# A fourth buffer of split weights, and the tiles that make room for it, in a one-core decoder block

## The chip, the core and the metric

The kernel runs on one core of one Trainium2 chip. The core has a matrix engine (PE; its weight loads are shown apart as PEld), a vector engine (DVE), an activation engine (ACT), a general engine (POOL), and a sync engine whose queue (SP) issues the transfers from memory. Each engine works through its own instructions in the order in which they stand. The metric is the device time of one execution in microseconds (us), the median of several runs. The profiled execution is one more of them, and its trace names start, end and releaser of each instruction.

## The reference: what is computed

One decoder layer over 256 tokens of width 2048, all in float32:

```python
xn = rms_norm(h, norm_mix_g)
proj = xn @ w_in                      # 2048 -> 1024 + 1024 + 3*1024 + 3*2048
u_s5, u_lru, q, k, v, gate_logits = split(proj)
gates = sigmoid(gate_logits + b_gate)
y_s5   = s5_branch(u_s5, ...)         # complex diagonal recurrence, 64 groups x 64 states, GELU, GLU
y_lru  = rglru_branch(u_lru, ...)     # causal conv, two block-diagonal gates, real recurrence
y_attn = stick_breaking_attention(q, k, v)   # 8 heads of 128
merged = g_s5*(y_s5 @ w_br_s5) + g_lru*(y_lru @ w_br_lru) + g_attn*(y_attn @ w_br_attn)
h = h + merged @ w_out
hn = rms_norm(h, norm_mlp_g)
h = h + relu(hn @ w_up)**2 @ w_down   # 2048 -> 8192 -> 2048
return rms_norm(h, final_norm_g)
```

In the S5 branch the state turns by a fixed angle per step, so the kernel needs cosine and sine of (frequency x step) for 256 steps of each state.

## The kernel before, in words

**Units.** All large weights are read once, as a stream of 520 units. A unit is 256 rows by 512 columns of one weight matrix, 512 KB, held in a tile of 128 partitions by 1024 elements. `stream` lists them in the order of their use: first `w_in` for the LRU and S5 inputs, then gates and branch products, attention inputs, the S5 tail with `w_glu`, `w_out`, and last `w_up` and `w_down`.

**Split weights.** To keep float32 accuracy in a faster matmul form, every unit is split in two: ACT casts the raw tile to a rounded `hi` (line 146), DVE subtracts to get `lo` (line 147). Activations are split the same way. A product is then three matmuls: hi by hi, hi by lo, lo by hi. `chunk` (lines 225 to 227) makes the output with channels on the partitions, 24 matmuls of 256 columns per unit; `chunk_tok` (lines 241 to 243) and `pair_tok` (lines 276 to 278) make it with tokens on the partitions, 12 matmuls of 512 columns per unit.

**How far ahead.** `next_unit` is called before the matmuls of unit i. It issues loads up to unit i+3 into one of three `raw` buffers (pool `wraw`), and splits up to unit i+2 into one of three pairs of `hi` and `lo` buffers (pool `whi`). The split of unit i+2 therefore waits until PE has done with unit i-1, whose buffers it takes, and the load of a unit waits until the split of the unit three before it has freed its `raw` buffer. A load waiting in SP's queue holds up everything behind it there.

**Side work.** All else runs between the units. After each unit's matmuls `pump` takes a step of every open side task: the norms, the LRU branch (`lru_half`), the S5 branch (`s5_scan`), attention, the transposes of the feed-forward part. `pump` ties these steps behind the newest split on ACT and DVE and behind the unit's last matmul on PE; within such bounds a scheduler sets each engine's order when the program is built. So the number of splits that stand ahead of a side step on its engine is given by how far ahead the splits are issued.

**The S5 branch.** `s5_params` computes the angles on POOL: a per-state frequency, split in a low part (per step) and a high part (per 16 steps), and from them two tables `flo` and `fhi` of 128 x 32 x 16 each. `s5_scan` goes through 8 blocks of 4 state tiles. For each block it splits the input into `ux`, copies it by 12 small transfers (`s5_stack`, line 627) into `stk`, multiplies (`ps_v`), turns by the tables from `s5_tables` (lines 604 to 611: a DVE sum of `fhi` and `flo`, then ACT and DVE make cosine and sine `tc` and `ts`), scans, turns back, and multiplies again (`ps_y`, line 698). After the eighth block come GELU and the split into `yg_hi` and `yg_lo`, which the `w_glu` chunks read.

**Memory.** Tile pools give out memory. Tiles of one tag share that tag's buffers: a new tile of the tag waits until the old one is released, that is until its last reader is done. `wr` and `wi` (the LRU's block-diagonal gate weights) lie in the LRU's pool, `stk` in the S5 pool, `vt` (attention values) under its own tag, and `x_tok` and `ho` (residual input, output rows) side by side in the feed-forward pool.

Of the kernel before, what the change touches and what calls it, by code (L numbers as in the profile page):

```python
# [9 lines left out]
F32 = mybir.dt.float32  # L10
F32R = mybir.dt.float32r
AF = mybir.ActivationFunctionType
ALU = mybir.AluOpType
# [33 lines left out]
def hybrid_block(ctx: ExitStack, tc: tile.TileContext, io, out):  # L47
# [2 lines left out]

    const = ctx.enter_context(tc.tile_pool(name="const", bufs=1))
    wraw = ctx.enter_context(tc.tile_pool(name="wraw", bufs=3))
    whi = ctx.enter_context(tc.tile_pool(name="whi", bufs=3))
    act = ctx.enter_context(tc.tile_pool(name="act", bufs=1))
    ypool = ctx.enter_context(tc.tile_pool(name="ypool", bufs=2))
    tmp = ctx.enter_context(tc.tile_pool(name="tmp", bufs=2))
# [94 lines left out]
    def next_unit():  # L151
        i = st["use"]
        st["use"] += 1
        while st["load"] <= min(i + 3, len(stream) - 1):
            load_next()
            load_x(st["load"])
        while st["split"] <= min(i + 2, len(stream) - 1):
            before_split(st["split"])
            split_next()
        return (stream[i], *hi.pop(i))  # L160
# [147 lines left out]
    bco = sp.tile([P, WT, 2, 64], F32, name="bco")  # L308
    ce = sp.tile([P, 2, 32, 2, 16], F32, name="ce")
    ux = sp.tile([P, 4, L], F32R, name="ux")  # L310
    stk = sp.tile([96, NT, 2, L], F32R, name="stk")
    rad = sp.tile([P, 32], F32, name="rad")
    fhi = sp.tile([P, 32, 16], F32, name="fhi")
    flo = sp.tile([P, 32, 16], F32, name="flo")
    pp = s5.enter_context(tc.tile_pool(name="s5w", bufs=1))


# [94 lines left out]
    def s5_params():  # L412
        lr, li, dt, a, b, n, w, den, sh, ch, ea, em, xr, xi, cr, ci = (prm[:, k, :] for k in range(16))
        g = nc.gpsimd
        g.memset(ce, 0.0)
        for _ in range(9):
            yield
        nc.scalar.activation(dt, dt, AF.Exp)
        yield
        g.tensor_tensor(b, li, dt, ALU.mult)  # L420
        g.tensor_tensor(a, lr, dt, ALU.mult)
        g.tensor_scalar(n, b, 1.0 / TWO_PI, MAGIC, ALU.mult, ALU.add)
        g.tensor_scalar(n, n, -MAGIC, None, ALU.add)
        for cst in (PI_A, PI_B, PI_C):
            g.tensor_scalar(w, n, cst, None, ALU.mult)
            g.tensor_tensor(b, b, w, ALU.subtract)
        g.tensor_scalar(b, b, math.pi, -math.pi, ALU.min, ALU.max)
        yield
        g.tensor_scalar(w, b, 1.0 / TWO_PI, None, ALU.mult)
        g.tensor_scalar(n, w, 16.0, MAGIC, ALU.mult, ALU.add)  # L430
        g.tensor_scalar(n, n, -MAGIC, None, ALU.add)
        g.tensor_scalar(cr, w, 16.0, None, ALU.mult)
        g.tensor_tensor(n, cr, n, ALU.subtract)
        sb = steps.unsqueeze(1).broadcast_to([P, 32, 16])
        g.tensor_tensor(flo, w.unsqueeze(2).broadcast_to([P, 32, 16]), sb, ALU.mult)
        g.tensor_tensor(fhi, n.unsqueeze(2).broadcast_to([P, 32, 16]), sb, ALU.mult)
        yield
        nc.scalar.activation(ch, b, AF.Abs)
        nc.scalar.activation(sh, b, AF.Sin, scale=0.5)
        nc.scalar.activation(ch, ch, AF.Sin, scale=-0.5, bias=half_pi)  # L440
        nc.scalar.activation(ea, a, AF.Exp)
        nc.scalar.activation(em, a, AF.Tanh, scale=0.5)
        g.tensor_tensor(den, lr, lr, ALU.mult)
        g.tensor_tensor(w, li, li, ALU.mult)
        g.tensor_tensor(den, den, w, ALU.add)
        yield
        nc.vector.reciprocal(den, den)
        g.tensor_scalar(n, sh, 2.0, None, ALU.mult)
        g.tensor_tensor(xi, n, ch, ALU.mult)
        g.tensor_tensor(w, ea, em, ALU.mult)  # L450
        g.tensor_tensor(em, em, w, ALU.add)
        g.tensor_scalar(rad, em, 1.0, None, ALU.add)
        g.tensor_tensor(n, n, sh, ALU.mult)
        g.tensor_tensor(n, n, ea, ALU.mult)
        g.tensor_tensor(xr, em, n, ALU.subtract)
        g.tensor_tensor(xi, xi, ea, ALU.mult)
        yield
        g.tensor_tensor(cr, xr, lr, ALU.mult)
        g.tensor_tensor(w, xi, li, ALU.mult)
        g.tensor_tensor(cr, cr, w, ALU.add)  # L460
        g.tensor_tensor(cr, cr, den, ALU.mult)
        g.tensor_tensor(ci, xr, li, ALU.mult)
        g.tensor_tensor(w, xi, lr, ALU.mult)
        g.tensor_tensor(ci, ci, w, ALU.subtract)
        g.tensor_tensor(ci, ci, den, ALU.mult)
        yield
        cb_, ib_ = (x.unsqueeze(2).broadcast_to([P, 32, 16]) for x in (cr, ci))
        for k, (p, q, op) in enumerate(((cb_, ib_, ALU.add), (ib_, cb_, ALU.subtract))):
            u = pp.tile([P, 2, 32, 16], F32, tag="ts", name=f"cq{k}", bufs=2)
            nc.vector.tensor_tensor(u[:, 0], cco[:, 0], p, ALU.mult)  # L470
            yield
            nc.vector.tensor_tensor(u[:, 1], cco[:, 1], q, ALU.mult)
            yield
            for h in range(2):
                r_ = slice(64 * h, 64 * h + 64)
                nc.vector.tensor_tensor(ce[r_, k, :, h, :], u[r_, 0], u[r_, 1], op)
                yield
# [14 lines left out]
    nsp8 = const.tile([P, WT], F32, name="nsp8")  # L492
    tiny = const.tile([P, 1], F32, name="tiny")
    nc.gpsimd.memset(tiny, 2.0 ** -115)
    wr = lp.tile([P, WT, P], F32, name="wr")
    wi = lp.tile([P, WT, P], F32, name="wi")
    for t, src in ((wr, "lru_w_r"), (wi, "lru_w_i")):
        nc.gpsimd.memset(t, 0.0)

# [95 lines left out]
    def s5_tables(b):  # L595
        c = pp.tile([P, NT, 16, 16], F32, tag="tc", name=f"tc{b}", bufs=2)
        s = pp.tile([P, NT, 16, 16], F32, tag="ts", name=f"ts{b}", bufs=2)
        q = slice(b * NT, (b + 1) * NT)
        sh = [P, NT, 16, 16]
        f = "p n a b -> p (n a b)"  # L600
        cf, sf = c.rearrange(f), s.rearrange(f)

        def gen():
            nc.vector.tensor_tensor(c, fhi[:, q, :].unsqueeze(3).broadcast_to(sh), flo[:, q, :].unsqueeze(2).broadcast_to(sh), ALU.add)
            yield
            nc.scalar.activation(sf, cf, AF.Identity, bias=magic)
            nc.vector.scalar_tensor_tensor(sf, sf, -MAGIC, cf, ALU.add, ALU.subtract)
            yield
            nc.scalar.activation(cf, sf, AF.Abs)
            nc.scalar.activation(sf, sf, AF.Sin, scale=-TURN)  # L610
            nc.scalar.activation(cf, cf, AF.Sin, scale=-TURN, bias=half_pi)
            yield
        f = "p n a b -> p n (a b)"
        return (c.rearrange(f), s.rearrange(f)), gen()

    def s5_split(ct):
        bx = [ux[:, 2 + i, :].rearrange("p (r g s) -> p r g s", r=2, g=2) for i in range(2)]
        nc.scalar.copy(ux[:, 0, :], us5[:, ct, :])
        nc.vector.tensor_tensor(ux[:, 1, :], us5[:, ct, :], ux[:, 0, :].bitcast(F32), ALU.subtract)
        for g in range(2):  # L620
            m = mask[:, g:g + 1]
            nc.scalar.activation(bx[0][:, :, g, :], bco[:, ct], AF.Copy, scale=m)
            nc.vector.scalar_tensor_tensor(bx[1][:, :, g, :], bco[:, ct], m, bx[0][:, :, g, :].bitcast(F32), ALU.mult, ALU.subtract)

    def s5_stack(t):
        for i, w_ in enumerate((ux[:, 0:4:2, :], ux[:, 1:3, :], ux[:, 0:4:3, :])):
# [4 lines left out]
    def s5_scan():  # L631
# [12 lines left out]
        for b in range(WT):  # L644
# [11 lines left out]
            if b + 1 < WT:  # L656
                s5_split(b + 1)
                tabs, more = s5_tables(b + 1)
                yield
            tt(t1, vr, c, ALU.mult)  # L660
            yield
            tt(t2, vi, s, ALU.mult)
# [172 lines left out]
    for c in range(2):  # L835
        kT = ap_.tile([P, 4, L], F32, tag="k", name=f"kT{c}")
        banks = chunk("w_in", 6 + c, D, xs)
        for j in range(2):
            scaled(kT[:, 2 * j:2 * j + 2, :], banks[j])
        qT = ap_.tile([P, 4, L], F32, tag="q", name=f"qT{c}")  # L840
        banks = chunk("w_in", 4 + c, D, xs)
        for j in range(2):
            nc.vector.scalar_tensor_tensor(qT[:, 2 * j:2 * j + 2, :], v2(banks[j]), P ** -0.5, rstd2, ALU.mult, ALU.mult)
        vbox = [None]
        tasks.append(later([attention(range(4 * c, 4 * c + 4), kT, qT, vbox)], 1.0))
        banks = chunk_tok("w_in", 8 + c, D, xs)
        vt = ap_.tile([P, 2, CH], F32, tag="v", name=f"vt{c}")
        for t in range(2):
            nc.scalar.activation(vt[:, t, :], banks[t], AF.Copy, scale=rstd_tok[:, t:t + 1])
        vbox[0] = vt  # L850
        if c == 0:
            finish(tasks[0])
# [67 lines left out]

    mlp = ctx.enter_context(tc.tile_pool(name="mlp", bufs=1))
    gp = small("norm_mlp_g")
    x_tok = mlp.tile([P, 2, D], F32, name="xres")

    def x_load():
        for c in range(4):
# [71 lines left out]


    gfb = mlp.tile([P, D], F32, name="gfb")  # L1000
    ho = mlp.tile([P, 2, D], F32, name="ho")
    ssq = mlp.tile([P, 2, 6], F32, name="ssq")
    rf = mlp.tile([P, 2], F32, name="rf")

# [166 lines left out]
```

## Time and profile before

| what | value |
|---|---|
| median of 3 runs | 1511.09 us (1510.91 to 1512.21) |
| the profiled execution: time, and span of its trace | 1512.1 us, 1510.3 us |
| mean granted PE clock over the span | 0.995 |
| PE busy | 1488.4 us, 99% |
| DVE busy | 1175.2 us, 78% |
| ACT busy | 782.3 us, 52% |
| POOL busy | 35.3 us, 2% |
| bytes moved, mean rate | 292.41 MB, 194 GB/s |

Busy PE means that a matmul is on its way, from its start to its modelled end; matmuls overlap, so the mean duration of one (389 ns for 512 columns) is longer than the distance from one to the next. A stall shows as idle time of PE and of PEld with its releaser, and as a gap between starts. The granted clock is a share of full speed: a stretch at 0.86 ran its matmuls as if 14% of it were lost.

### The profile page before, as it was taken

Reading aid. Unit: us, or ns where it says so; the run is one execution under the profiler, and the core shown is the slowest. Engines: PE = TensorE matmul, PEld = TensorE weight load, DVE = VectorE, ACT = ScalarE, POOL = GpSimd, SP = SyncE. Lnnn points to the kernel's source line nnn. Section 1 sums busy time; section 2 is a strip of 40 time slices with the busy share of each in tenths; the row PEclk is TensorE's granted clock in tenths of the full one; section 3 lists DMA queues with packets and bytes.
Section 4 is the critical chain, followed back from the end, with each engine's and each line's share of the span. In section 5 each row is a group of like instructions: output and inputs, shape, how many; then the busy total and the mean of one; then the engine's idle time right before and its main releaser. Section 6 shows DMA issues by size and latency. Waiting matters only on the chain.

```text
span 1510.3 us, 19900 instructions
## 1 busy us (share of the span) xinstructions
PE 1488.4 (99%) x7518; PEld 1260.5 (83%) x7518; DVE 1175.2 (78%) x1468; ACT 782.3 (52%) x920; POOL 35.3 (2%) x60
## 2 busy tenths in 40 slices
PE   9999999999999999999999999999999999999997
PEld 9997788989887878988887888888888888888886
DVE  6767998897988989689799796568854787558965
ACT  6767556565765564544455544344433444344443
POOL 1400000000000000000000000000000000000011
PEclk9999999999999999999999999999999999999999
DMA  9546766665555666666855666666666666666664
GB/s 287 157 153 176 228 205 201 187 182 168 175 172 183 208 182 210 189 202 190 276 182 188 197 184 205 194 185 196 198 194 193 193 195 195 195 191 191 192 197 152
DMA packets 89858, 292.41 MB, mean 194 GB/s; under 512 B 12834, under 2 KB 17058, under 8 KB 89634
## 3 DMA queue, kind: packets, MB, share of 16 engines
q1 hardware_dynamic: 89618, 291.07, 62.6%
q8 instruction: 59, 0.97, 0.3%
q14 instruction: 37, 0.30, 0.1%
q10 hardware_dynamic: 144, 0.07, 0.0%
HBM read 282.71 MB, written 2.10 MB: 189 GB/s over the span
## 4 chain that ended last, share of the span: by engine, by line
PE 83%; DVE 9%; issue 3%; ACT 2%; DMA 2%; SPq 0%; DVEq 0%; ACTq 0%
PE mt_w_up L242 6%; PE mt_w_up L241 6%; PE mt_w_up L243 6%; PE mt_w_in L242 5%; PE mt_w_in L243 5%; PE mt_w_in L241 5%; PE mt_w_down L242 4%; PE mt_w_down L241 4%; PE mt_w_down L243 4%; PE mp_w_down L277 4%; PE mp_w_down L278 4%; PE mp_w_down L276 4%; PE mm_w_in L227 4%; PE mm_w_in L225 4%; PE mm_w_in L226 4%; DVE lo L147 3%
## 5 line engine op out<-in xcount | busy, mean ns | idle before, releaser
L146 ACT CAST hi<-raw 128x1024 fp32r<-128x1024 f32 (+1 forms) x521 | 545.2, 1049 | 625.9 <-PE mt_w_up L243 131.4
L147 DVE TENSOR_TENSOR lo<-raw,hi 128x1024 fp32r<-128x1024 f32 (+1 forms) x521 | 637.9, 1225 | 287.7 <-ACT hi L146 284.1
L242 PE MATMUL mt_w_in<-lo,xhi 128*128 128x512 f32 x448 | 176.1, 393 | 3.9 <-DVE lo L147 3.7
L241 PE MATMUL mt_w_in<-hi,xhi 128*128 128x512 f32 x448 | 175.2, 396 | 0.2 <-ACT hi L146 0.2
L243 PE MATMUL mt_w_in<-hi,xlo 128*128 128x512 f32 x448 | 175.2, 391 | 0.0
L241 PE MATMUL mt_w_up<-hi,hhi 128*128 128x512 f32 x448 | 174.3, 389 | 0.0
L242 PE MATMUL mt_w_up<-lo,hhi 128*128 128x512 f32 x448 | 174.3, 389 | 0.0
L243 PE MATMUL mt_w_up<-hi,hlo 128*128 128x512 f32 x448 | 174.3, 389 | 0.0
L227 PE MATMUL mm_w_in<-xhi,lo 128*128 128x256 f32 x512 | 145.4, 286 | 4.5 <-DVE lo L147 4.5
L225 PE MATMUL mm_w_in<-xhi,hi 128*128 128x256 f32 x512 | 146.5, 286 | 0.5 <-ACT hi L146 0.4
L226 PE MATMUL mm_w_in<-xlo,hi 128*128 128x256 f32 x512 | 145.7, 285 | 0.0
L728 DVE STREAM_TRANSPOSE reluT<-relu 32x256 f32<-32x256 f32 x256 | 111.5, 436 | 4.2
L242 PEld LDWEIGHTS mt_w_in<-lo,xhi 128*128 128x128 f32 x448 | 84.6, 189 | 24.0 <-DVE lo L147 7.6
L227 PEld LDWEIGHTS mm_w_in<-xhi,lo 128*128 128x128 f32 x512 | 98.7, 194 | 5.5 <-DVE lo L147 5.5
L242 PE MATMUL mt_w_down<-lo,hd_hi 128*128 128x512 f32 (+1 forms) x272 | 102.5, 377 | 0.0
L241 PE MATMUL mt_w_down<-hi,hd_hi 128*128 128x512 f32 (+1 forms) x272 | 102.4, 377 | 0.0
L243 PE MATMUL mt_w_down<-hi,hd_lo 128*128 128x512 f32 (+1 forms) x272 | 102.4, 376 | 0.0
L225 PEld LDWEIGHTS mm_w_in<-xhi,hi 128*128 128x128 f32 x512 | 99.2, 194 | 1.1 <-ACT hi L146 1.0
L277 PE MATMUL mp_w_down<-lo,hd_hi 128*128 128x512 f32 x256 | 99.8, 390 | 0.1
L278 PE MATMUL mp_w_down<-hi,hd_lo 128*128 128x512 f32 x256 | 99.6, 389 | 0.0
L276 PE MATMUL mp_w_down<-hi,hd_hi 128*128 128x512 f32 x256 | 99.6, 389 | 0.0
L241 PEld LDWEIGHTS mt_w_in<-hi,xhi 128*128 128x128 f32 x448 | 84.5, 189 | 17.8 <-ACT hi L146 0.7
(299 smaller groups left out, 2370.2 us busy)
## 6 DMA issues: line engine op xcount, KB each, us to landing
raw<-in_w_in SPq DMA_DIRECT2D x175, 512.0 KB, 4.3
raw<-in_w_up SPq DMA_DIRECT2D x128, 512.0 KB, 4.2
raw<-in_w_down SPq DMA_DIRECT2D x128, 512.0 KB, 4.2
raw<-in_w_out SPq DMA_DIRECT2D x32, 512.0 KB, 4.2
raw<-in_w_br_lru SPq DMA_DIRECT2D x16, 512.0 KB, 4.6
raw<-in_w_br_attn SPq DMA_DIRECT2D x16, 512.0 KB, 4.1
raw<-in_w_br_s SPq DMA_DIRECT2D x16, 512.0 KB, 4.1
stk<-ux SPq DMA_DIRECT2D x96, 64.0 KB, 4.1
```

The costliest lines, as they stand in the source:

```text
L146: anchor["act"] = nc.scalar.copy(h[:, k, :], r[:, k, :]).ins
L147: anchor["dve"] = nc.vector.tensor_tensor(l_[:, k, :], r[:, k, :], h[:, k, :].bitcast(F32), ALU.subtract).ins
L225: nc.tensor.matmul(o, wh[:, kk, s], xh, start=first and ct % 2 == 0, stop=False, skip_group_check=True)
L226: nc.tensor.matmul(o, wh[:, kk, s], xl, start=False, stop=False, skip_group_check=True)
L227: mm = nc.tensor.matmul(o, wl[:, kk, s], xh, start=False, stop=last and ct % 2 == 1, skip_group_check=True)
L241: nc.tensor.matmul(banks[j], xh[:, s], wh[:, a:b], start=kt == 0, stop=False)
L242: nc.tensor.matmul(banks[j], xh[:, s], wl[:, a:b], start=False, stop=False)
L243: return nc.tensor.matmul(banks[j], xl[:, s], wh[:, a:b], start=False, stop=kt == ng * UK - 1)
L276: nc.tensor.matmul(o, xh[:, s], wh[:, kk, :], start=kt == 0, stop=False)
L277: nc.tensor.matmul(o, xh[:, s], wl[:, kk, :], start=False, stop=False)
L278: mm = nc.tensor.matmul(o, xl[:, s], wh[:, kk, :], start=False, stop=kt == ng * UK - 1)
L728: nc.vector.transpose(d_[32 * a:32 * a + 32, :, :, 32 * b:32 * b + 32], s_[32 * b:32 * b + 32, :, :, 32 * a:32 * a + 32])
```

## The change

Six edits.

- The pool `whi` has four pairs of `hi` and `lo` buffers in place of three.
- `next_unit` loads four units ahead in place of three, and splits three ahead in place of two. The pool `wraw` stays at three buffers.
- `wr` and `wi` become halves of one tile `wrwi` in the S5 pool under the tag `stk`, and `stk` is allocated later under the same tag, so it takes this memory once the LRU's last gate matmul has read it.
- `fhi` and `flo` go. Their two frequency columns stay in `fw` (128 x 2 x 32), and for each S5 block POOL multiplies 4 of them by the 16 steps into a tile `ph` (two instructions of 128 x 64 per block), one step of the generator before DVE's sum. So `s5_tables` has one step more.
- `vt` takes the tag of `kT`: it waits for the logits of its four heads, and the next `kT` waits for the products that read `vt`.
- `x_tok` and `ho` share one buffer under the tag `rows`.

```diff
-    whi = ctx.enter_context(tc.tile_pool(name="whi", bufs=3))
+    whi = ctx.enter_context(tc.tile_pool(name="whi", bufs=4))
...
-        while st["load"] <= min(i + 3, len(stream) - 1):
+        while st["load"] <= min(i + 4, len(stream) - 1):
...
-        while st["split"] <= min(i + 2, len(stream) - 1):
+        while st["split"] <= min(i + 3, len(stream) - 1):
...
-    stk = sp.tile([96, NT, 2, L], F32R, name="stk")
-    fhi = sp.tile([P, 32, 16], F32, name="fhi")
-    flo = sp.tile([P, 32, 16], F32, name="flo")
+    fw = sp.tile([P, 2, 32], F32, name="fw")
...
+        w = fw[:, 0, :]
         g.tensor_scalar(w, b, 1.0 / TWO_PI, None, ALU.mult)
...
-        g.tensor_tensor(n, cr, n, ALU.subtract)
-        sb = steps.unsqueeze(1).broadcast_to([P, 32, 16])
-        g.tensor_tensor(flo, w.unsqueeze(2).broadcast_to([P, 32, 16]), sb, ALU.mult)
-        g.tensor_tensor(fhi, n.unsqueeze(2).broadcast_to([P, 32, 16]), sb, ALU.mult)
+        g.tensor_tensor(fw[:, 1, :], cr, n, ALU.subtract)
...
-    wr = lp.tile([P, WT, P], F32, name="wr")
-    wi = lp.tile([P, WT, P], F32, name="wi")
+    wrwi = sp.tile([P, 2, WT, P], F32, tag="stk", name="wrwi")
+    wr, wi = wrwi[:, 0], wrwi[:, 1]
...
-            nc.vector.tensor_tensor(c, fhi[:, q, :].unsqueeze(3).broadcast_to(sh), flo[:, q, :].unsqueeze(2).broadcast_to(sh), ALU.add)
+            ph = pp.tile([P, 2, NT, 16], F32, tag="ph", name=f"ph{b}")
+            for k in range(2):
+                nc.gpsimd.tensor_tensor(ph[:, k], fw[:, k, q].unsqueeze(2).broadcast_to([P, NT, 16]),
+                                        steps.unsqueeze(1).broadcast_to([P, NT, 16]), ALU.mult)
+            yield
+            nc.vector.tensor_tensor(c, ph[:, 1].unsqueeze(3).broadcast_to(sh), ph[:, 0].unsqueeze(2).broadcast_to(sh), ALU.add)
...
+    stk = sp.tile([P, NT, 2, L], F32R, tag="stk", name="stk")[0:96]
...
+            next(more, None)
             tt(t1, vr, c, ALU.mult)
...
-        vt = ap_.tile([P, 2, CH], F32, tag="v", name=f"vt{c}")
+        vt = ap_.tile([P, 2, CH], F32, tag="k", name=f"vt{c}")
...
-    x_tok = mlp.tile([P, 2, D], F32, name="xres")
+    x_tok = mlp.tile([P, 2, D], F32, tag="rows", name="xres")
...
-    ho = mlp.tile([P, 2, D], F32, name="ho")
+    ho = mlp.tile([P, 2, D], F32, tag="rows", name="ho")
```

The order in which the built programs issue their instructions moves with it. Units are numbered by their place in the stream: `hi31` and `raw31` belong to unit 31.

**ACT, in the LRU's second half**, where the gates' sigmoids (lines 545 and 546, now 542 and 543) and what follows them stand between the casts (line 146). The rows begin at unit 31's cast and end at the first cast behind the block. Before:

```order
L146 CAST hi31_1303<-raw31_1255 128x1024
L555 ACT_TABLE_LOAD
L555 ACTIVATE lru_r1_1070<-lru_r1_1070,nsp8_143 128x256
L545 ACT_TABLE_LOAD
L545 ACTIVATE lru_tc1_1073<-ps_l1_6_1285,par_79 128x256
...
L550 ACTIVATE lru_ts1_1074<-lru_tc1_1073,sp4_142 128x256 x2
L555 ACT_TABLE_LOAD
L555 ACTIVATE lru_r1_1070<-lru_r1_1070,nsp8_143 128x256
L555 ACTIVATE lru_tc1_1073<-lru_tc1_1073,nsp8_143 128x256 x2
L146 CAST hi32_1337<-raw32_1301 128x1024
```

and after:

```order
L146 CAST hi31_1259<-raw31_1217 128x1024
L547 ACTIVATE lru_th1_1074<-lru_r1_1072,sp4_140 128x256 x2
L146 CAST hi32_1305<-raw32_1257 128x1024
L542 ACTIVATE lru_tc1_1075<-ps_l1_6_1287,par_79 128x256
...
L547 ACTIVATE lru_ts1_1076<-lru_tc1_1075,sp4_140 128x256 x2
L552 ACT_TABLE_LOAD
L552 ACTIVATE lru_r1_1072<-lru_r1_1072,nsp8_141 128x256 x2
L552 ACTIVATE lru_tc1_1075<-lru_tc1_1075,nsp8_141 128x256 x2
L146 CAST hi33_1339<-raw33_1303 128x1024
```

The long block stood ahead of unit 32 and now stands ahead of unit 33, and two of its three table loads are gone.

**ACT, at the S5 table of block 6**, which fell together with the sigmoids of an attention gate (`gate2_1`). Before:

```order
L146 CAST hi150_4654<-raw150_4623 128x1024
L609 ACTIVATE tc6_4380<-ts6_4381 128x1024
L610 ACT_TABLE_LOAD
L610 ACTIVATE ts6_4381<-ts6_4381 128x1024
L751 ACT_TABLE_LOAD
L751 ACTIVATE gate2_1_0_4644<-gate2_1_0_4644 128x512
L751 ACTIVATE gate2_1_1_4647<-gate2_1_1_4647 128x512
L611 ACT_TABLE_LOAD
L611 ACTIVATE tc6_4380<-tc6_4380,half_pi_131 128x1024
L146 CAST hi151_4676<-raw151_4652 128x1024
```

and after:

```order
L146 CAST hi151_4674<-raw151_4645 128x1024
L756 ACTIVATE gate2_1_0_4664<-gate2_1_0_4664 128x512
L756 ACTIVATE gate2_1_1_4667<-gate2_1_1_4667 128x512
L608 ACTIVATE ts6_4427<-tc6_4426,magic_131 128x1024
L146 CAST hi152_4695<-raw152_4672 128x1024
L611 ACTIVATE tc6_4426<-ts6_4427 128x1024
L146 CAST hi153_4717<-raw153_4693 128x1024
L612 ACT_TABLE_LOAD
L612 ACTIVATE ts6_4427<-ts6_4427 128x1024
L613 ACTIVATE tc6_4426<-tc6_4426,half_pi_129 128x1024
L146 CAST hi154_4737<-raw154_4715 128x1024
```

The gate's two sigmoids went ahead of the table, the casts of units 152 and 153 went in between, and one table load stands where three stood.

**DVE, at the end of the S5 branch**: `us5` takes the last block's `ps_y`, `g1_7` is its GELU, `yg_lo` is what the `w_glu` matmuls read. Before:

```order
L147 TENSOR_TENSOR lo192_5598<-raw192_5577,hi192_5597 128x1024
L700 SCALAR_TENSOR_TENSOR us5_99<-us5_99,par_79,ps_y7_5613 128x256
L147 TENSOR_TENSOR lo193_5626<-raw193_5595,hi193_5625 128x1024
L711 SCALAR_TENSOR_TENSOR g1_7_5641<-g1_7_5641,us5_99 128x512
...
L714 SCALAR_TENSOR_TENSOR us5_99<-g1_7_5641,us5_99 128x512
L147 TENSOR_TENSOR lo194_5669<-raw194_5623,hi194_5668 128x1024
L875 SCALAR_TENSOR_TENSOR yg_lo_5653<-us5_99,yg_hi_5652 128x512
```

and after:

```order
L147 TENSOR_TENSOR lo194_5642<-raw194_5621,hi194_5641 128x1024
...
L705 SCALAR_TENSOR_TENSOR us5_99<-us5_99,par_79,ps_y7_5657 128x256
L147 TENSOR_TENSOR lo195_5695<-raw195_5639,hi195_5694 128x1024
L716 SCALAR_TENSOR_TENSOR g1_7_5673<-g1_7_5673,us5_99 128x512
L719 SCALAR_TENSOR_TENSOR us5_99<-g1_7_5673,us5_99 128x512
L147 TENSOR_TENSOR lo196_5725<-raw196_5692,hi196_5724 128x1024
L880 SCALAR_TENSOR_TENSOR yg_lo_5679<-us5_99,yg_hi_5678 128x512
```

The S5 step moved behind two more splits, where the LRU's block above moved behind one; on PE its `ps_y` moved from 12 matmuls ahead of the first `w_glu` matmul to directly ahead of it.

More of the change, by code (lines that the diff above doesn't have):

```diff
@@ L432, in s5_params @@
         g.tensor_scalar(cr, w, 16.0, None, ALU.mult)
-        g.tensor_tensor(n, cr, n, ALU.subtract)
-        sb = steps.unsqueeze(1).broadcast_to([P, 32, 16])
-        g.tensor_tensor(flo, w.unsqueeze(2).broadcast_to([P, 32, 16]), sb, ALU.mult)
-        g.tensor_tensor(fhi, n.unsqueeze(2).broadcast_to([P, 32, 16]), sb, ALU.mult)
+        g.tensor_tensor(fw[:, 1, :], cr, n, ALU.subtract)
+        w = prm[:, 6, :]
         yield
```

## The prediction

> **What bounds the kernel now.** I read the first part of the page, then what PE waits for, then busy time and clock by stretch.
>
> ```profile
> PE 1488.4 (99%) x7518; PEld 1260.5 (83%) x7518; DVE 1175.2 (78%) x1468; ACT 782.3 (52%) x920; POOL 35.3 (2%) x60
> PE mm_w_in L227 <- DVE lo L147: 4.5, 5, 1.9
> PE mt_w_in L242 <- DVE lo L147: 3.7, 5, 1.9
> PE mt_w_br_attn L241 <- ACT hi L146: 2.2, 1, 2.2
> PE mp_w_up L277 <- DVE lo L147: 0.9, 1, 0.9
> ```
>
> PE is busy for 99%, so the matmuls are the bound, and the change leaves their number alone. All that can be had is the time in which PE lacks a split unit: the four rows of waits (total us, times, longest) name nothing but casts and subtractions. Two steady stretches give PE's pace (us, then PE busy and matmuls, and so on; last the clock, the DMA share and GB/s):
>
> ```profile
> 12.00:40.00 28.00, 28.00 (x236) 28.00 (x235) 22.06 (x31) 18.58 (x28) 3.54 (x6) 1.00 0.97 289
> 920.00:1320.00 400.00, 400.00 (x1766) 331.21 (x1765) 266.45 (x313) 172.23 (x172) 0.00 (x0) 1.00 0.63 194
> ```
>
> 28.00/236 = 0.119 us per 256-column matmul, 400/1766 = 0.2265 us per 512-column one: a unit lasts 24 x 0.119 = 2.85 us or 12 x 0.2265 = 2.72 us. One unit more ahead is worth that much lateness. The stretches with stalls, in the same columns:
>
> ```profile
> 40.00:52.00 12.00, 10.24 (x82) 9.78 (x82) 8.96 (x18) 9.94 (x17) 8.72 (x21) 1.00 0.42 133
> 84.00:96.00 12.00, 9.82 (x68) 9.41 (x67) 12.00 (x21) 5.65 (x8) 0.00 (x0) 0.86 0.51 140
> 112.00:136.00 24.00, 21.08 (x93) 16.63 (x92) 20.45 (x27) 20.06 (x26) 0.00 (x0) 0.93 0.47 134
> 136.00:172.00 36.00, 35.36 (x157) 28.44 (x156) 27.44 (x30) 17.59 (x22) 0.00 (x0) 1.00 0.76 225
> 456.00:464.00 8.00, 7.61 (x33) 5.77 (x32) 8.00 (x9) 2.12 (x3) 0.00 (x0) 1.00 0.60 171
> 480.00:492.00 12.00, 9.63 (x35) 7.23 (x34) 7.94 (x7) 7.03 (x9) 0.00 (x0) 0.86 0.43 138
> 804.00:812.00 8.00, 7.06 (x31) 5.18 (x30) 7.99 (x12) 5.63 (x8) 0.00 (x0) 1.00 0.52 173
> ```
>
> Idle PE, row by row: 1.76, 2.18, 2.92, 0.64, 0.39, 2.37, 0.94, together 11.2 us. Three rows also show a lower clock: 0.14 x 12 = 1.7, 0.07 x 24 = 1.7, 0.14 x 12 = 1.7, together 5.1 us. And each wait costs a little beyond its idle time, as PE starts anew:
>
> ```profile
> 90.10 0.28 PE L226 MATMUL mm_w_in<-xlo,hi 128*128 128x256 f32 x1
> 92.31 0.42 PE L227 MATMUL mm_w_in<-xhi,lo 128*128 128x256 f32 x1 [1.93 <-DVE lo L147]
> ```
>
> From start to start 2.21 us where the pace is 0.12: 2.09 lost, 1.93 of it idle, so 0.16 more. The rows of waits above count 12, and some shorter stops of the weight loads add a few: about 14 x 0.16 = 2.2. In all 11.2 + 5.1 + 2.2 = 18.5 us hang on late splits.
>
> **The change part by part: the fourth buffer.** It helps where the splitter was ahead as far as its buffers let it, then fell behind one burst of side work. That it usually is buffer-bound shows in what the casts wait for:
>
> ```profile
> ACT hi L146 <- PE mt_w_up L243: 131.4, 86, 1.7
> ACT hi L146 <- DMA raw<-in_w_in: 61.5, 39, 3.0
> ACT hi L146 <- DMA raw<-in_w_in: 6.8, 4, 2.6
> ```
>
> The first row is a wait for a freed buffer; the second a wait for a load, which a fourth pair doesn't shorten. The third row is the stretch 28:44, ahead of the first stall: there the loads were the limit.
>
> Stall by stall, with idle, clock and 0.16 per wait. At 40:52: 1.76 + 0.3 = 2.1. At 84:96: 2.18 + 1.7 + 0.3 = 4.2; the lateness itself, 2.18, is under 2.85, so it goes, and I let the clock loss go with it. At 456: 0.39 + 0.16 = 0.55. At 804: 0.94 + 0.16 = 1.1. At 480:492 the late cast stood behind this on ACT:
>
> ```profile
> 473.81 1.06 ACT hi L146
> ...
> 478.20 1.28 ACT L751
> ...
> 480.65 1.28 ACT L611
> ...
> 483.10 1.89 ACT hi L146 x2
> ```
>
> The chain of waits has no cast from 474.9 to 483.1, 8 us. In the new order casts stand between, and two table loads of 1.28 are gone, so 2.37 + 1.7 + 0.3 = 4.4 goes. The stretch 112:172 is the hard one: 2.92 + 0.64 + 1.7 and some six waits, 6.2 us, is more than a unit, and the splitter doesn't get ahead in between. It begins with this ACT block:
>
> ```profile
> 103.85 1.05 ACT L146 CAST hi<-raw 128x1024 fp32r<-128x1024 f32 x1
> 104.92 1.28 ACT L555 ACT_TABLE_LOAD   x1
> 106.74 1.28 ACT L545 ACT_TABLE_LOAD   x1
> 109.12 0.48 ACT L546 ACTIVATE lru_ts<-ps_l,par 128x256 f32<-128x256 f32 x1
> 110.41 1.28 ACT L555 ACT_TABLE_LOAD   x1
> 112.92 1.03 ACT L146 CAST hi<-raw 128x1024 fp32r<-128x1024 f32 x1
> ```
>
> A unit of slack gives 2.7 there. Two table loads fewer are 2.6 us of ACT, of which I count half, as DVE and the loads are late there too: 2.7 + 1.3 = 4.0, between 2.7 and 6.2. Sum: 2.1 + 4.2 + 0.55 + 1.1 + 4.4 + 4.0 = 16.35 us.
>
> From the table of waits I take nothing for the feed-forward part: PE has no wait there to lose.
>
> **The phases on POOL.** Two products of 128x512 go, sixteen of 128x64 come. The nearest rows:
>
> ```profile
> L435 POOL TENSOR_TENSOR flo<-prm,par 128x512 f32<-128x512 f32 x1 | 1.1, 1064 | 0.1
> 54.25 0.25 POOL L459 TENSOR_TENSOR prm<-prm 128x32 f32<-128x32 f32 x1
> 43.13 0.43 DVE L347 SCALAR_TENSOR_TENSOR rs<-rs 128x256 f32<-128x256 f32 x1 [2.84 <-ACT rs L346]
> 44.12 1.01 DVE L349 SCALAR_TENSOR_TENSOR rstd<-rs,rs 128x256 f32<-128x256 f32 x1
> 43.78 1.06 POOL L435 TENSOR_TENSOR flo<-prm,par 128x512 f32<-128x512 f32 x1
> ```
>
> 128x64 lies close to the 128x32 row: 0.25 + 0.81 x 32/480 = 0.3 us. POOL has nothing else then, and the product is issued a step ahead of DVE's sum. But DVE pays: `rstd` took 1.01 where an equal form took 0.43, while POOL's 1.06 ran, 0.58 more. So 16 POOL instructions hold DVE for 16 x 0.3 = 4.8 us, at most 16 x 0.58 = 9.3, over the S5 blocks. That lies under PE's work except where DVE is the late engine, the first block at 152:172: two instructions, 0.6 us, bounds 0 and 1.2. Without its cover all 9.3 would count. The Trainium skill (SBUF — State Buffer, "Who interferes with whom") says the same: a DVE instruction with two SBUF inputs and a GpSimd instruction that reads SBUF lock each other out for a whole instruction. The rows agree; by the rule alone, were DVE the bound throughout, this change would lose up to those 9.3 us.
>
> **Shared buffers.** The first transfer into `stk`:
>
> ```profile
> 129.14 0.72 SPq L627 DMA_DIRECT2D stk<-ux  x1
> ```
>
> It now waits for the last LRU gate matmul, whose result ACT read at 109.12 (row above), 20 us earlier: nothing. `vt` waits for the logits of its heads, which stand units ahead on PE, `ho` for `x_tok`, read before the feed-forward part begins: nothing. If `stk` did wait on SP, it would hold the loads behind it; that is in the last rival.
>
> **Sum.** 16.35 - 0.6 = 15.7 us. The profiled execution took 1512.1 (span 1510.3), so 1496.4; the median of the runs lies 1.0 below it, 1511.09 - 15.7 = **1495.4 us**.
>
> **The rivals.**
>
> *Slack fills only partly (1502).* Each stall returns one unit at most and the clock stays lost in part; at 40:52 nothing, as the loads limit there: 2.7 (84) + 2.7 (112) + 0.55 + 2.7 (480) + 1.1 - 0.6 = 9.1, so 1511.1 - 9.1 = 1502. For it: the load waits. Against: at 480 and 112 the order itself got shorter.
>
> *The clock falls anyway (1499).* The clock losses at 84 and 480, 3.4 us, stay: 15.7 - 3.4 = 12.3, so 1498.8. Against it: each dip follows a stall near 2 us, and the 1.76 us at 40:52, in two pieces, drew none. The Trainium skill (TensorE: Matmul & The Clock Gate, Part 1) lets the clock fall to half only after an idle window of about 3.4 us; stalls of 2.2 us would by that not cause the dips. The trace speaks against it: 0.86 in both stretches.
>
> *All of it returns (1492.6).* 1511.1 - 18.5. For it: the table loads gone from the two worst blocks. Against it: at 136:172 PE still loses 0.64 us after the burst is over, so slack doesn't come back there. Beyond this lies what only the weight loads show:
>
> ```profile
> PEld mt_w_in L242 <- DVE lo L147: 7.6, 9, 2.3
> ```
>
> 7.6 us where PE's own row has 3.7. The 3.9 between them are mostly under matmuls still on their way, so they aren't in the sum; they set the lower end, 1492.6 - 3.9 = 1488.7.
>
> *Nothing moves (1511).* The three `raw` buffers stay, and if the loads set the splitter's pace the fourth pair stays empty. Against it: the first row of cast waits.
>
> *Slower: the S5 chain becomes the bound (1517).* Its steps now stand behind two more splits, its table has one step more, its `stk` transfers wait on SP, and its last `ps_y` stands a unit closer to `w_glu`.
>
> ```profile
> 601.36 0.48 DVE L700 SCALAR_TENSOR_TENSOR us<-us,par,ps_y 128x256 f32<-128x256 f32 x1 [1.44 <-PE ps_y L698]
> 607.01 0.69 DVE L875 SCALAR_TENSOR_TENSOR yg_lo<-us,yg_hi 128x512 fp32r<-128x512 f32 x1 [0.21 <-ACT yg_hi L874]
> L226 PE MATMUL mm_w_glu<-yg_lo,hi x64: 282/283/283, 604.2 to 626.9; 128*128 128x256 f32 x64
> ```
>
> `yg_lo` was done at 607.7 and its last slices are read three units into `w_glu`, at 604.2 + 3 x 2.85 = 612.8: 5.1 us spare, 2.4 if the end comes a unit later. From there on every us late is a us lost. A unit late in each of 8 blocks is 8 x 2.72 = 21.8, against a gain of 15.7: 1517. Against it: only the last block's lateness reaches PE, and the spare is not used up.
>
> **How the numbers follow.** Forecast 0.52, partly filled 0.18, clock 0.05, all 0.13, nothing 0.06, slower 0.06. The forecast's own range is 1491 to 1499 (112:172 at its bounds, POOL at its bounds, a stall more or less). The range for 8 in 10 takes in the partly filled and the full case with its lower end, 1489 to 1503. What a measurement of this kernel can tell from no change is about 0.2%, 3 us: faster 0.88, same 0.06, slower 0.06.
>
> **What would show it.** Right: PE's waits for `lo` and `hi` fall from 11 us to 2 or 3, those left lie between 112 and 172; the clock is 1.00 at 84:96 and 480:492; casts wait longer for PE than before. Wrong: waits left at 40:52 and load waits of the casts grown (partly filled); clock dips without a stall; PE waiting for `yg_lo`, `ps_v` or `ps_y` (S5 chain); DVE's S5 sums lengthened by over 0.58 us each.

## The result, and the profile after

The changed kernel takes 1496.34 us at the median (1494.38 to 1496.72); before, run beside it, takes 1511.61 (1510.91 to 1512.21). The ratio is 0.9897, 95% interval 0.9881 to 0.9913: 15.3 us faster, where 15.7 were forecast. The profiled execution took 1496.72 us, its span is 1495.0.

What PE waits for after the change (total us, times, longest):

```profile
PE ps_y L703 <- DVE s_t L697: 1.8, 1, 1.8
PE mm_w_in L227 <- DVE lo L147: 1.4, 2, 0.8
PE mm_w_in L225 <- ACT hi L146: 1.2, 2, 0.7
PE mp_w_up L277 <- DVE lo L147: 0.8, 1, 0.8
PE ps_v L654 <- DVE us L705: 0.6, 1, 0.6
```

The waits for `hi` and `lo` fell from 11.3 us in the prediction's rows to 3.4. Two rows are new, and both are steps of S5. The prediction's stretches after the change (length, PE busy and matmuls, weight loads, DVE, ACT, POOL; last clock, DMA share, GB/s):

```profile
40.00:52.00 12.00, 12.00 (x101) 11.95 (x101) 9.15 (x20) 9.66 (x16) 7.81 (x24) 1.00 0.55 182
84.00:96.00 12.00, 11.17 (x88) 10.78 (x86) 12.00 (x21) 5.05 (x9) 0.00 (x0) 1.00 0.46 148
112.00:136.00 24.00, 24.00 (x109) 19.79 (x109) 21.14 (x28) 19.49 (x24) 2.98 (x2) 1.00 0.63 194
136.00:172.00 36.00, 36.00 (x162) 29.68 (x161) 30.71 (x35) 19.16 (x25) 4.12 (x2) 1.00 0.79 234
172.00:200.00 28.00, 26.20 (x123) 20.29 (x122) 23.38 (x25) 17.47 (x21) 0.00 (x0) 0.94 0.59 196
480.00:492.00 12.00, 11.39 (x66) 8.72 (x65) 9.63 (x13) 7.53 (x12) 0.00 (x0) 1.00 0.67 220
804.00:812.00 8.00, 8.00 (x37) 6.62 (x36) 7.72 (x14) 3.49 (x4) 0.00 (x0) 1.00 0.51 156
```

Of the idle time in these stretches before 172, 0.83 us is left. The largest new loss is in one place, 172:200: 1.80 us idle, and 0.06 x 28 = 1.7 us of lower clock. The same stretch before has neither:

```profile
172.00:200.00 28.00, 27.99 (x136) 22.22 (x136) 25.52 (x28) 17.82 (x19) 0.00 (x0) 1.00 0.67 211
```

There PE reads the results of S5 block 0 for the sixteen products `ps_y`; the last eight need DVE's last sum. Before, from the timeline (start, us, engine, line):

```profile
193.84 1.22 DVE L147 TENSOR_TENSOR lo<-raw,hi 128x1024 fp32r<-128x1024 f32 x1
194.98 1.22 DVE L692 TENSOR_TENSOR s_t<-s_t,s_v 128x1024 f32<-128x1024 f32 x1
...
196.05 1.07 PE L698 MATMUL ps_y<-s_t,ce 128*32 128x256 f32 x16
```

and after:

```profile
186.88 0.64 PE L703 MATMUL ps_y<-s_t,ce 128*32 128x256 f32 x8
...
187.46 1.22 DVE L147 TENSOR_TENSOR lo<-raw,hi 128x1024 fp32r<-128x1024 f32 x1
...
188.59 1.22 DVE L697 TENSOR_TENSOR s_t<-s_t,s_v 128x1024 f32<-128x1024 f32 x1
...
189.87 1.08 PE L703 MATMUL ps_y<-s_t,ce 128*32 128x256 f32 x8 [1.79 <-DVE s_t L697]
```

PE arrives 196.05 - 186.88 = 9.2 us earlier than before, DVE's last sum starts only 194.98 - 188.59 = 6.4 us earlier. Before, that sum ended at 196.20, when the first eight of the sixteen products were running: the margin was below half of the sixteen's 1.07 us, so what PE gained on DVE up to there beyond that had to show. In both traces each of the chain's last three DVE instructions stands behind a `lo`, 1.1 us apiece.

### The profile page after: what moved, and what is told of

It is laid out like the page before. It is cut to its first block, busy times and chain, and to the rows that moved or that the text cites. A ratio compares the mean times of both kernels' runs of the same rounds, so it can differ in the third digit from the quotient of the medians.

```text
span 1495.0 us, 19909 instructions
## 1 busy us (share of the span) xinstructions
PE 1479.8 (99%) x7518; PEld 1258.0 (84%) x7518; DVE 1174.3 (79%) x1468; ACT 775.5 (52%) x916; POOL 52.9 (4%) x74
## 4 chain that ended last, share of the span: by engine, by line
PE 76%; DVE 13%; DMA 4%; issue 3%; ACT 2%; POOL 0%; SPq 0%; DVEq 0%; ACTq 0%
PE mt_w_up L242 7%; PE mt_w_up L241 7%; PE mt_w_up L243 7%; DVE lo L147 5%; PE mt_w_in L241 5%; PE mt_w_in L242 5%; PE mt_w_in L243 5%; PE mp_w_down L278 4%; PE mp_w_down L276 4%; PE mp_w_down L277 4%; PE mt_w_down L242 4%; PE mt_w_down L241 4%; PE mt_w_down L243 4%; PE mm_w_in L227 3%; PE mm_w_in L226 3%
## 5 line engine op out<-in xcount | busy, mean ns | idle before, releaser
L243 PEld LDWEIGHTS mt_w_in<-hi,xlo 128*128 128x128 f32 x448 | 84.3, 188 | 17.7
L241 PEld LDWEIGHTS mt_w_up<-hi,hhi 128*128 128x128 f32 x448 | 84.1, 188 | 17.5
```

The lines of the kernel that those rows point to most:

```text
L241: nc.tensor.matmul(banks[j], xh[:, s], wh[:, a:b], start=kt == 0, stop=False)
L243: return nc.tensor.matmul(banks[j], xl[:, s], wh[:, a:b], start=False, stop=kt == ng * UK - 1)
```

## Experiments

The line numbers in the rows are those of each run's own code. Ratios are to before, run beside each; an interval reaches about 0.15%, 2 us, to either side, so a smaller difference between two experiments shows nothing by itself.

**1. The change without its fourth buffer.**

```diff
-    whi = ctx.enter_context(tc.tile_pool(name="whi", bufs=4))
+    whi = ctx.enter_context(tc.tile_pool(name="whi", bufs=3))
...
-        while st["load"] <= min(i + 4, len(stream) - 1):
+        while st["load"] <= min(i + 3, len(stream) - 1):
...
-        while st["split"] <= min(i + 3, len(stream) - 1):
+        while st["split"] <= min(i + 2, len(stream) - 1):
```

> The change without its fourth buffer: three buffers of split weights, splits two units ahead, loads three; the phases on GpSimd with their own step, and the shared tiles, stay. My theory (the buffer and the look-ahead returned the 16.35 us, the phases cost 0.6): the time of before plus 0.6, 1512 us (1510 to 1514), PE's waits for lo and hi again near 11 us, and no wait for ps_y near 190 us, since late splits leave VectorE its time. Rival A (the phase edit itself makes the new wait for ps_y): that wait of 1.8 us with its clock dip stands here too, and the time is 1515. Rival B (part of the gain comes from the other edits, which move the table loads about): 1508 or less.

1505.09 us, ratio 0.9963 (0.9948 to 0.9978). Rival B: some 6 us came without the buffer. There is no wait for `ps_y`, so the phases alone don't make it. The stretches at 112 and 480:

```profile
112.00:136.00 24.00, 22.30 (x102) 17.69 (x102) 21.28 (x28) 20.27 (x25) 2.99 (x2) 1.00 0.55 169
480.00:492.00 12.00, 11.53 (x65) 8.63 (x64) 11.15 (x13) 6.31 (x8) 0.00 (x0) 1.00 0.52 167
```

At 480:492 it lost 0.47 us where before lost 2.37 and the clock, though nothing there was split any earlier.

**2. Four buffers, look-ahead as before.**

```diff
-        while st["load"] <= min(i + 4, len(stream) - 1):
+        while st["load"] <= min(i + 3, len(stream) - 1):
...
-        while st["split"] <= min(i + 3, len(stream) - 1):
+        while st["split"] <= min(i + 2, len(stream) - 1):
```

> The change with four buffers, but splits two units ahead and loads three, as before. My theory (a late cast stands in ScalarE's order behind a block of side work, so what counts is how far ahead it stands in that order): about the time of before plus 0.6, 1512 us, at best 1508, with the waits for lo and hi at 84:96 and 480:492 still there. Rival (the casts of before waited 131 us for a freed buffer, so the buffer alone lets them run ahead): 1503 or less, and those waits are gone.

1497.67 us, ratio 0.9913 (0.9898 to 0.9928). My expectation was wrong by 14 us, the rival right on the time: without any longer look-ahead the casts move forward. Some 6 us of it belong to the step, though (experiment 5), and not all waits went: 84:96 still has 1.93 us idle, against 0.83 with the look-ahead.

**3. The change without the price of its phases, step and products.**

```diff
+    ph = pp.tile([P, 2, NT, 16], F32, name="ph")
+    def s5_phase0():
+        for k in range(2):
+            nc.gpsimd.tensor_tensor(ph[:, k], fw[:, k, 0:NT].unsqueeze(2).broadcast_to([P, NT, 16]),
...
-            ph = pp.tile([P, 2, NT, 16], F32, tag="ph", name=f"ph{b}")
-            for k in range(2):
-                nc.gpsimd.tensor_tensor(ph[:, k], fw[:, k, q].unsqueeze(2).broadcast_to([P, NT, 16]),
-                                        steps.unsqueeze(1).broadcast_to([P, NT, 16]), ALU.mult)
-            yield
...
+        s5_phase0()
         tabs, more = s5_tables(0)
...
-            next(more, None)
             tt(t1, vr, c, ALU.mult)
```

> The change without the price of its phases: the two small products are made once, for block 0, and all eight blocks read them, so the phases of blocks 1 to 7 are not computed (sines and cosines of wrong angles, same amount of work); the generator has no step for them, as before. Left out are 14 GpSimd products and 8 steps. My theory (GpSimd holds VectorE in the first block alone, 0.6 us, and the new wait for ps_y comes from splits three units ahead): the time after less 0.6, 1495.7 us, with the wait for ps_y near 188 us still there. Rival A (the added step or GpSimd makes that wait): the wait is gone, 1492.4 us or less. Rival C (GpSimd costs VectorE nothing): 1496.3, the same wait.

1496.84 us, ratio 0.9906 (0.9889 to 0.9922): no difference from the change. PE still waits for `ps_y`, now 1.0 us and without a dip of the clock, so the step isn't what makes that wait. And buffer and look-ahead by themselves take 14.2 to 14.5 us off before, where the prediction gave them 16.35.

**4. One more empty step ahead of `ps_y` in block 0.**

```diff
-            yield
-            yield
+            for _ in range(2 + (b == 0)):
+                yield
             ps = pss.tile([P, CH], F32, tag="ps", name=f"ps_y{b}")
```

> The change with one more empty step before the output products of the first S5 block, so that ps_y of block 0 stands one unit later on PE. In the trace after, PE waits there 1.8 us at 188 us for VectorE's last sum, and runs at half clock for some 2 to 3 us behind it; from start to start about 4 us are lost there. My theory (VectorE is just late by less than a unit): the wait and the dip go and nothing takes their place, 1496.3 - 3.9 = 1492.4 us (1491.5 to 1494). Rival (VectorE has too much to do up to there, so the next thing behind it is late instead): a wait for lo, ps_v or ps_y appears between 190 and 200, and the time stays at 1495 or more.

1492.88 us, ratio 0.9885 (0.9869 to 0.9900): by the medians 3.5 us below the change, as idle and clock of 172:200 add up to (1.80 + 1.7). The intervals overlap, and one of its four executions took 1496.38; what the trace shows is that the wait is gone: the stretch reads 27.92 of 28.00 at clock 1.00. Experiment 9 measures the edit beside the change.

**5. Before, with one empty step more in each table.**

```diff
         def gen():
+            yield
             nc.vector.tensor_tensor(c, fhi[:, q, :].unsqueeze(3).broadcast_to(sh), flo[:, q, :].unsqueeze(2).broadcast_to(sh), ALU.add)
...
+            next(more, None)
             tt(t1, vr, c, ALU.mult)
```

> Before with one edit: each S5 block's tables get one more, empty step, at the place where the change puts the phases. Buffers, look-ahead, tiles and the two large GpSimd products stay as before; the work is the same, only its order on the engines moves. My theory now (what the change gained with three buffers, 6.2 us, came from the step: it shifts S5's pieces against the splits and so breaks up the blocks ahead of the waits at 112:136 and 480:492): 1505 us (1503.5 to 1507), PE without loss at 480:492 but for 0.5 us, and the wait at 90 us still there. Rival (the gain came from the shared tiles or from the two large products gone from GpSimd at 43 us): 1511, as before.

1504.25 us, ratio 0.9959 (0.9944 to 0.9973). An edit that computes nothing gives what the first experiment left unexplained, so neither the shared tiles nor the shorter work on POOL did. Apart from POOL and the names of tiles, its engines' orders are those of experiment 1. Where it shows:

```profile
136.00:172.00 36.00, 36.00 (x163) 29.63 (x162) 29.09 (x33) 18.90 (x24) 0.00 (x0) 1.00 0.77 236
480.00:492.00 12.00, 11.61 (x66) 8.75 (x65) 11.16 (x13) 6.33 (x9) 0.00 (x0) 1.00 0.52 165
```

The step moves all that S5 issues against the casts, and at 480 it breaks up the block that stood ahead of the late cast: ACT casts in it, at 472.8 and 475.6 us, and has one table load there in place of three. The LRU's block ahead of 112 it leaves as it was, against my expectation:

```profile
102.47 1.05 ACT L146 CAST hi<-raw 128x1024 fp32r<-128x1024 f32 x1
103.55 1.28 ACT L555 ACT_TABLE_LOAD   x1
...
105.37 1.28 ACT L545 ACT_TABLE_LOAD   x1
...
109.04 1.28 ACT L555 ACT_TABLE_LOAD   x1
...
111.55 2.92 ACT L146 CAST hi<-raw 128x1024 fp32r<-128x1024 f32 x3
```

112:136 still loses 24 - 21.81 = 2.19 us here, though without the dip. Over all runs, the block at 480 is broken up wherever the step is in, and the LRU's block loses two of its three table loads wherever splits stand three ahead (experiment 3, the change and its variants); experiments 1, 2, 5 and 6 keep them.

**6. The fourth buffer alone**, with neither look-ahead nor step: experiment 3's edit, and

```diff
-        while st["load"] <= min(i + 4, len(stream) - 1):
+        while st["load"] <= min(i + 3, len(stream) - 1):
...
-        while st["split"] <= min(i + 3, len(stream) - 1):
+        while st["split"] <= min(i + 2, len(stream) - 1):
```

> The change with four buffers, splits two units ahead and loads three as before, and no step for the phases (products made once, for block 0, and read by all blocks; wrong angles in blocks 1 to 7): the fourth buffer alone. The step alone took 6.5 us off before, the buffer on top of the step 7.4 more, buffer and look-ahead without the step 14.8. My theory (buffer and step remove the same waits in part, so they don't add up): the buffer alone returns most of it, 1499 us (1496 to 1502). Rival (each removes its own waits): 1511.3 - 7.4 = 1504 us (1502.5 to 1506).

1503.47 us, ratio 0.9950 (0.9937 to 0.9962). The rival: each removes its own waits. With three buffers the step gives 0.41%, without the step the buffer gives 0.50%, and together they give 0.87% (experiment 2). What the buffer leaves without the step is above all the stretch at 112, dip of the clock and all (84:96 keeps 2.07 us idle, 480:492 0.47):

```profile
112.00:136.00 24.00, 20.80 (x81) 16.18 (x82) 20.25 (x26) 18.53 (x23) 0.00 (x0) 0.93 0.52 156
```

**7. The price of POOL's products.** As experiment 3, but both places of the step stay:

```diff
-            ph = pp.tile([P, 2, NT, 16], F32, tag="ph", name=f"ph{b}")
-            for k in range(2):
-                nc.gpsimd.tensor_tensor(ph[:, k], fw[:, k, q].unsqueeze(2).broadcast_to([P, NT, 16]),
-                                        steps.unsqueeze(1).broadcast_to([P, NT, 16]), ALU.mult)
             yield
```

> The change with its step kept, but the two small products made once, for block 0, and read by all eight blocks: 14 GpSimd products less, wrong angles in blocks 1 to 7, and the order of the other engines as in the change. What it differs from the change by is the price of GpSimd's products. By the prediction 0.6 us of them reach PE: 1495.7. My theory now (GpSimd waits for VectorE, not VectorE for it, since the products lasted 1.27 us at the median and 0.29 at the least while VectorE's sums stayed at 1.22): no difference, 1496.3 (1495.3 to 1497.3), the wait for ps_y at 188 us still there. Rival (VectorE was held 0.58 us by each): 1492 to 1494, and that wait gone.

1495.55 us, ratio 0.9901 (0.9886 to 0.9916), with PE's wait for `ps_y` still 1.7 us. To place the difference of 0.8 us, it ran again beside the change itself:

> The changed kernel once more, unedited, as the measure for the three runs beside it on the same chip: 1496.3 us (1494.4 to 1496.8), a ratio to before of 0.990.

> The change without 14 of its 16 GpSimd products, all engines' order else the same (wrong angles in blocks 1 to 7), beside the change itself on the same chip. What is open is 0.8 us between 1495.55 and 1496.34, taken at different times. My theory (GpSimd's products cost the others nothing): within 0.7 us of the change. The prediction's price: 0.6 us less. Rival (VectorE held 0.58 us each time): 2 us less or more.

The change: 1495.85 (ratio 0.9902, 0.9887 to 0.9917); without the products: 1495.16 (0.9896, 0.9882 to 0.9909). Twice some 0.7 us lower, which fits the 0.6 forecast and isn't told from nothing, as each kernel's runs spread by 2 us. 2 us or more is not seen.

**8. Loads five ahead.**

```diff
-        while st["load"] <= min(i + 4, len(stream) - 1):
+        while st["load"] <= min(i + 5, len(stream) - 1):
```

> The change with loads five units ahead instead of four; splits stay three ahead, and the three buffers for loads stay. My theory (after the change the loads are not what PE waits for: its waits for lo and hi are 3.4 us, at 0:12, at 90 us and at 796 us, where VectorE and ScalarE are late): 1496.3 (1495.3 to 1497.3). Rival (the casts' longer waits for loads, 80 us against 62 before, show that loads now limit): the waits for lo and hi fall to 1 us, 1494 or less.

1496.98 us (1494.49 to 1499.38), ratio 0.9910 (0.9895 to 0.9925): no gain, as expected, though the waits for `hi` and `lo` did fall, to 1.8 us. In their place:

```profile
PE ps_v L654 <- DMA stk<-ux: 2.0, 2, 1.8
```

The transfers into `stk` stand on SP behind the loads: here two load transfers are issued right ahead of the second three of them, where the change has one ahead of each two, and the slowest took 6.4 us from issue to landing (5.6 in the change). That is the mechanism that the prediction put into its slower rival; the change itself has no such wait.

**9. One more step in blocks 0 and 6.**

```diff
-            yield
-            yield
+            for _ in range(2 + (b in (0, 6))):
+                yield
```

> The change with one more empty step before the output products of S5 blocks 0 and 6. With block 0 alone it took 1492.9 us, and its largest loss left was a wait of 1.1 us for ps_y of block 6 at 535 us. My theory (each such wait is less than a unit): that wait goes too, 1492.9 - 1.2 = 1491.7 us (1490.8 to 1493). Rival (the end of the S5 chain stands a unit later again, and the subtraction yg_lo is then late for w_glu): a wait for yg_lo near 590 us, and 1492.9 or more.

> The change with one more empty step before the output products of S5 blocks 0 and 6, beside the change itself on the same chip. My theory (two waits of PE for ps_y go, 3.5 and 1.7 us by the runs so far): 5.2 us below the change, ratio to before 0.987 with an interval that ends below that of the change. Rival (the two differ by no more than the scatter between executions): under 2 us apart.

1491.18 us, ratio 0.9873 (0.9857 to 0.9890), and again 1491.59, 0.9873 (0.9860 to 0.9887), while the change beside it took 1495.85. So it is 4.3 us faster than the change, where 5.2 were expected, and 19 to 20 faster than before, the fastest kernel here; its interval ends at the edge of that of the change, 0.9887. What PE still waits for:

```profile
PE mm_w_in L227 <- DVE lo L147: 1.2, 2, 0.7
PE warm L327 <- POOL eps_t L336: 1.0, 1, 1.0
PE mm_w_in L225 <- ACT hi L146: 0.7, 1, 0.7
```

## Why the prediction was right, step by step

**Bound and cause: right.** The matmuls are the same, and the time that came back and can be placed is time in which PE lacked a split unit, or ran slower behind such a wait. Buffer and look-ahead alone bring it (experiment 3). The buffer alone gives 7.2 us (experiment 6), 7.4 on top of the step (experiments 1 and 2). The look-ahead gives 6.6 more without the step (experiments 6 and 3) and only 1.3, within the scatter, with it (experiment 2 and the change), where the S5 wait of 3.5 us that it brings takes most of it back. The look-ahead with three buffers was not run.

**The stalls, term by term.** 40:52 and 456:464 returned whole, as forecast. 84:96: 4.2 forecast, 2.18 - 0.83 + 1.7 = 3.05 measured.

804:812: 1.1 forecast, and it looks as if it had returned, as the stretch after is full. But PE is 12 us earlier there by then, and the stall went with it: the same `h_tok` on DVE, a late `lo` behind it, one unit further on. Before, then after:

```profile
806.65 1.28 DVE L971 TENSOR_TENSOR h_tok<-mt_w_out,xres 128x512 f32<-128x512 f32 x2
807.85 1.22 DVE L147 TENSOR_TENSOR lo<-raw,hi 128x1024 fp32r<-128x1024 f32 x1
809.13 0.50 PE L277 MATMUL mp_w_up<-lo,hhi 128*128 128x512 f32 x1 [0.90 <-DVE lo L147]
```

```profile
794.67 1.28 DVE L976 TENSOR_TENSOR h_tok<-mt_w_out,xres 128x512 f32<-128x512 f32 x2
795.87 1.21 DVE L147 TENSOR_TENSOR lo<-raw,hi 128x1024 fp32r<-128x1024 f32 x1
797.14 0.50 PE L277 MATMUL mp_w_up<-lo,hhi 128*128 128x512 f32 x1 [0.76 <-DVE lo L147]
```

So 0.14 us of this term came back.

480:492: 4.4 forecast, 2.37 - 0.61 + 1.7 = 3.5 measured, and the 0.61 left is no cast but S5's `ps_v`. The new order that the prediction counted on there comes from the step, which gives it with three buffers too (experiments 1 and 5). In experiment 3, which keeps the old order, the old block still holds up a unit, one further on: 0.85 us idle at 474 us.

112:172: 4.0 forecast, all of its 6.2 returned. That term was mis-sized: the sum gave the stretch one unit of slack and half of two table loads. Most of the rest came with the look-ahead, with which the LRU's block is shorter: 112:136 loses 2.24 us of idle time in experiment 2 and nothing in the change, 3.2 and the clock in experiment 6 and 0.68 in experiment 3. The step, which the prediction costed as a price alone, takes the remainder.

**The step that failed: "only the last block's lateness reaches PE".** The prediction measured the S5 chain's margin at its end, at `yg_lo`. Block 0's `ps_y` reached PE first, with 3.5 us (1.80 idle and 1.7 of clock; experiment 4 takes both away). Its margin before, below half a us, stood in the timeline of before, and the prediction left it out. At the chain's end the rival was about right on the move: from `yg_lo` to its last use there were 5.1 us before, and after

```profile
595.90 0.69 DVE L880 SCALAR_TENSOR_TENSOR yg_lo<-us,yg_hi 128x512 fp32r<-128x512 f32 x1
L226 PE MATMUL mm_w_glu<-yg_lo,hi x64: 283/283/283, 590.8 to 613.5; 128*128 128x256 f32 x64
```

590.8 + 8.55 - 596.6 = 2.75 us, where it gave 2.4. PE doesn't wait for it.

**Why the sum came out all the same.** By idle time and clock alone the change's gain is smaller than 15.3: PE's idle time fell from 1510.3 - 1488.4 = 21.9 us to

```profile
PE 1479.8 (99%) x7518; PEld 1258.0 (84%) x7518; DVE 1174.3 (79%) x1468; ACT 775.5 (52%) x916; POOL 52.9 (4%) x74
```

1495.0 - 1479.8 = 15.2, 6.7 less; the lower clock cost 3 x 1.7 before and 1.7 after, 3.4 less; 10.1 together. Restarts are 2.4 of the other 5: past the first 12 us, the trace of before has 20 stalls that leave PE idle, where the prediction counted about 14, and from start to start they lose 3.2 us more than their idle time; after, 5 stalls lose 0.8 more. What remains, some 3 us, is spread over many small gaps between matmuls, none of them a stall, and no run here places it.

It does not lie in the weight loads, whose waits fell far more than PE's:

```profile
PEld mt_w_in L242 <- DVE lo L147: 0.4, 2, 0.2
PEld mm_w_in L227 <- DVE lo L147: 1.9, 3, 1.0
```

The first row was 7.6, 3.9 us beyond PE's own row. But where a weight load of before waited for `lo` and PE did not fall idle, six times past the first 12 us, the next matmul's start was late by 0.2 us in all. The prediction left the 3.9 out as "mostly under matmuls still on their way", and that was right.

So the sum came out partly by luck. 112:172 returned 2.2 more than forecast, and some 3 us came back that no term holds; against that, 84:96, 480:492 and 804:812 returned 3 less, and the new S5 wait took 3.5.

**The phases.** -0.6 was forecast, 0 to 0.7 measured. But the mechanism differed. In the trace after, block 1's products and DVE at the same time:

```profile
120.27 0.69 DVE L570 TENSOR_TENSOR ylru_lo<-lru_xc,ylru_hi 128x512 fp32r<-128x512 f32 x1
120.43 2.98 POOL L603 TENSOR_TENSOR ph<-fw,par 128x64 f32<-128x64 f32 x2 [60.80 <-DVE tc L606]
120.87 1.22 DVE L147 TENSOR_TENSOR lo<-raw,hi 128x1024 fp32r<-128x1024 f32 x1
122.00 1.32 DVE L567 TENSOR_TENSOR_SCAN lru_tc<-lru_tc,lru_ts 128x256 f32<-128x256 f32 x2
L603 POOL TENSOR_TENSOR ph<-fw,par x16: 292/1270/2881, 46.7 to 454.6; 128x64 f32<-128x64 f32 x16
```

A product took 0.29 us at the least (the 0.3 that I had estimated) and 1.27 at the median: beside a busy DVE it is POOL's instruction that gets longer. DVE's subtraction in these rows kept its 1.22 us. The 0.58 us that `rstd` lost before was met where POOL had begun first. The Trainium skill (SBUF — State Buffer, "Who interferes with whom") has the two lock each other out; that agrees, and which of them pays depended here on which one was running.

**What was to show it.** Waits for `hi` and `lo` at 3.4 us, clock 1.00 at 84:96 and 480:492: as said. "Casts wait longer for PE": wrong.

```profile
ACT hi L146 <- PE mt_w_up L243: 119.5, 78, 1.7
ACT hi L146 <- DMA raw<-in_w_in: 80.2, 49, 4.7
```

The first fell from 131.4, the second rose from 61.5: a cast that need not wait for a buffer comes to its load earlier. That sign had been put down to the rival in which the loads limit. In experiment 8 loads a unit earlier took 1.6 us off the waits for `hi` and `lo`, and the wait for `stk` put 2.0 in their place, so more look-ahead for the loads gains nothing here. What it would gain without that wait was not run.

## What to carry to other kernels

When a bound engine is to run ahead of the others, list every chain that feeds it, with its margin at each place where the bound engine reads it, not only at the end; the smallest one is the next wait, and an empty step in the order can be enough to move it. In a kernel whose order comes from a step count or a scheduler, run the shift of order alone before crediting a resource: here an empty step was worth 6.5 us with three buffers, 5.8 with four (experiments 6 and 2), and nothing measurable with four and a longer look-ahead. And follow a stall by the unit it holds up, not by the clock: in a kernel that has gained 12 us it stands 12 us earlier, and the old stretch looks clean.

## What the runs showed of the hardware

The granted clock falls after stalls of about 2 us, but not after each. Over the 14 profiles, the first 20 us left out, 11 stalls lost 1.9 to 2.3 us from start to start of matmuls; behind 9 of them the clock fell, behind those of experiment 5 (2.09 us, at 89 us) and experiment 8 (1.92 us, at 134 us) it did not. Behind the 30 that lost 0.8 to 1.7 us it never did. Experiments 1 and 5 have the same stall at 90 us, first 1 and then 5:

```profile
91.56 0.46 PE L227 MATMUL mm_w_in<-xhi,lo 128*128 128x256 f32 x1 [1.92 <-DVE lo L147]
84.00:96.00 12.00, 9.78 (x67) 9.37 (x66) 12.00 (x21) 5.96 (x9) 0.00 (x0) 0.86 0.46 156
```

```profile
91.52 0.39 PE L227 MATMUL mm_w_in<-xhi,lo 128*128 128x256 f32 x1 [1.93 <-DVE lo L147]
84.00:96.00 12.00, 9.74 (x79) 9.33 (x79) 12.00 (x21) 6.44 (x9) 0.00 (x0) 1.00 0.45 156
```

With the same idle time, 67 matmuls ran in one and 79 in the other: 12 x 0.119 = 1.4 us. A dip is thus a price of some 1.4 us that a stall near 2 us paid in one profile and not in the other, and it is charged to the wrong cause if a single profile is read. In the change's dip at 191 us the matmuls of 512 columns start 0.43 us apart, against 0.2265 in steady pace, so it runs at about half speed, and a stretch of 12 us at 0.86 holds 0.14 x 12 / 0.5 = 3.4 us of it. The Trainium skill (TensorE: Matmul & The Clock Gate, Part 1) describes a free-running window of about 3.4 us. That agrees with the length of the dips, and with their coming behind one such stall and not behind the next. The idle time that it asks for, a whole such window, is more than these stalls had: the longest left PE idle for 2.15 us.
